# Splitting expert weights two to a call and further ahead, and the order of the scale in differential attention

## Chip, cores and metric

One NeuronCore of a Trainium2 chip runs the whole program in one launch. The metric is device microseconds (us) from the start to the end of one execution; the kernel before has a median of 4869.98 us in three runs. Engines are named as in the profile: PE (TensorE matmul), PEld (its weight loads), DVE (VectorE), ACT (ScalarE), POOL (GpSimd), SP (SyncE, which issues DMAs here).

## What is computed

Two model blocks follow one another. The first has two layers; a layer normalises 1024 tokens (and, in layer 0, a context of 256 tokens too), mixes them (gating, a Fourier mix, differential attention and neighbourhood attention), and runs an expert layer. The second block (a delta rule and latent attention) is not touched. What is touched:

```python
# differential attention, per head: two softmaxes, the second is weighted and subtracted
w = softmax(q0 @ k0.T) - lam * softmax(q1 @ k1.T);  y = w @ v
# expert-choice feed-forward, 16 experts, each takes the 128 grid tokens (and 32 context tokens) that rank highest
h = silu(x_sel @ w_gate[e]) * (x_sel @ w_up[e])
x[sel] += g2 * gate * (h @ w_down[e])
```

All is float32. A product with near-float32 accuracy is made on PE from three float32r products: an operand x is split into xh (x rounded to float32r) and xl (x - xh), and xh·wh + xh·wl + xl·wh is summed.

## The kernel before

The program is written with a tile framework that puts in the semaphores and chooses, at compile time, the order of the instructions on each engine by a priority (the order of the program text) and by readiness in its own model of time. An engine then runs its own list strictly in that order. A pool's `bufs` is the number of buffers behind one tile name; a new tile waits until the oldest one has been read for the last time.

**Experts** (`experts`, from L1110; once per layer, `ctx` is true in layer 0). Each of 16 experts has three 1024x1024 weight matrices, so three products per expert: gate, up and down. The order is: gate 0, up 0, and then for each e: gate e+1, down e, up e+1. `weight` (L1160) brings one half of a matrix: a raw tile `w` of 128 x 4 x 1024 (2 MB) from the SP queue, with three raw buffers (`wraw`, made in `run`), and its split into `wh` and `wl`, two buffers of half a matrix each. The split goes in four quarters of 128x1024: ACT rounds (`wh`, L1165), then DVE subtracts (`wl`, L1166), except for the fourth quarter, whose subtraction goes to POOL. `product` (L1169) calls `weight` at the start of each half, and so the split of a half stands in the program right before the matmuls that need it. In layer 0 the half first runs the context's columns: 16 matmuls that use a 32-column strip of PE each, on the raw float32 `w` (L1181, `ps_c`; the trace has two records for each, 32 per half). Then come the half's 24 main matmuls (L1187, `ps_m`, 512 columns; the trace merges them in pairs).

Around the products stand `fetch` (a gather of the expert's tokens by POOL, and `flip`: four PE transposes into `ps_t`, a rounding on ACT at L1133 and a subtraction on DVE at L1134), `silu` (L1191: ACT tanh and a DVE multiply, after gate), `hidden` (L1199: gate times up and its flip), and `scatter` (L1214: DVE scaling into `rd`, and an accumulating scatter by POOL). `run` (L1223) places their steps between the `yield`s of a product: in layer 0 a product has 16 yields, eight of them in the context's part.

PSUM has eight banks: three `m` tiles of two banks, one `c` and one `t`, in both layers.

**Differential attention** (`diff_unit`, L577). A unit is one head and 128 queries against 1280 keys (256 for the two context units). `a(m)`, for the two maps m = 0, 1, makes scores S on PE (L591), takes a row minimum from PSUM on DVE (`mx`, L592, 128x1280) and the exponential on ACT (L594, into `e0` or `e1`). `b` takes reciprocals (L598), a one-column weight `sm` by a scalar-tensor-tensor (STT, L599), scales `e1` by it (L600), all on DVE, and adds `e0` on POOL (L601). `c` transposes the result on PE (L615) and copies it on ACT; `d` multiplies by v. `units` (L554) is a software pipeline written by hand: in one step the newest unit does a(0), the one before it b, the newest a(1), older ones d and c. There are two S tiles in PSUM. Layer 0 has 40 units (8 of them over 256 keys), layer 1 has 32.

Of the kernel before, what the change touches and what calls it, by code (L numbers as in the profile page):

```python
# [23 lines left out]
NE = 16  # L24
# [38 lines left out]
class Kernel:  # L63
# [490 lines left out]
    def units(self, q, new, steps):  # L554

        for i, u in enumerate(new):
# [3 lines left out]
            if old[0]:  # L560
                old[0]["a"](0)
            if old[1]:
                old[1]["b"]()
            if old[0]:
                old[0]["a"](1)
            for x in (0, 1):
# [10 lines left out]
    def diff_unit(self, p, ps, V, Y, h, Z, t):  # L577
# [6 lines left out]
        def a(m):  # L584
            if m == 0:
                U["mx"] = p.tile([128, 2], F32, name="mx", bufs=4)
                U["sm"] = p.tile([128, 4], F32, name="sm", bufs=6)
            S = ps("S", 3).rearrange("p a b -> p (a b)")
            for c in range(0, nk, 512):
                n = min(512, nk - c)  # L590
                nc.tensor.matmul(S[:, c:c + n], Z[0][m][:, t * 128:(t + 1) * 128], Z[1][m][:, k0 + c:k0 + c + n], start=True, stop=True)  # L591
            nc.vector.tensor_reduce(U["mx"][:, m:m + 1], S[:, :nk], AX.X, OP.min)  # L592
            e = U[m] = p.tile([128, T], F32, name=f"e{m}", bufs=3)
            nc.scalar.activation(e[:, :nk], S[:, :nk], AF.Exp, scale=-1.0, bias=U["mx"][:, m:m + 1], accum_out=U["sm"][:, m:m + 1])  # L594

        def b():
            sm, w = U["sm"], U[1]
            nc.vector.reciprocal(sm[:, 2:4], sm[:, 0:2])  # L598
            nc.vector.scalar_tensor_tensor(sm[:, 3:4], sm[:, 3:4], self.nlam, sm[:, 0:1], op0=OP.mult, op1=OP.mult)  # L599
            nc.vector.tensor_scalar(w[:, :nk], w[:, :nk], sm[:, 3:4], None, op0=OP.mult)  # L600
            nc.gpsimd.tensor_add(w[:, :nk], w[:, :nk], U[0][:, :nk])  # L601
# [37 lines left out]
    def nbr_unit(self, p, ps, V, Y, h, H, i):  # L639
# [34 lines left out]

        def b():
            sm = U["sm"]
# [433 lines left out]
    def experts(self, l):  # L1110
# [4 lines left out]
        quarters = [x.rearrange("t (g c) -> (t g) c", g=4) for x in (self.hc, self.xc)]  # L1115
        with self.pool("ex") as p, self.banks("exps", m=3, c=1, t=1) as ps:
            g2 = p.tile([128, 1024], F32, name="g2")
# [41 lines left out]

            def weight(name, e, half):  # L1160
                w = self.wr.tile([128, 4, 1024], F32, name="w", tag="w")
                nc.sync.dma_start(w, A[name][l, e, half * 512:(half + 1) * 512].rearrange("(k p) f -> p k f", p=128))
                wh, wl = [p.tile([128, 4, 1024], F32R, name=f"w{b}", bufs=2) for b in "hl"]
                for k in range(4):
                    nc.scalar.activation(wh[:, k], w[:, k], AF.Copy)  # L1165
                    (nc.gpsimd if k == 3 else nc.vector).tensor_sub(wl[:, k], w[:, k], wh[:, k].bitcast(F32))  # L1166
                return w, wh, wl

            def product(U, key, x, name, e):  # L1169

                pm = U[key] = ps("m", 2)
                pc = None
                X = U[x]
                for half in range(2):
                    w, *W = weight(name, e, half)
                    if ctx and half == 0:
                        pc = U[key + "c"] = ps("c")
                    for k in range(4 if ctx else 0):
                        b = half * 4 + k
                        for g in range(4):  # L1180
                            nc.tensor.matmul(pc[g * 32:(g + 1) * 32, :256], U[x[0] + "cT"][:, b % 2 * 128 + b // 2 * 32:b % 2 * 128 + b // 2 * 32 + 32],  # L1181
                                             w[:, k, g * 256:(g + 1) * 256], start=b == 0, stop=b == 7)
                        yield
                    for k in range(4):
                        for q, (i, j) in enumerate(((0, 0), (0, 1), (1, 0))):
                            for c in range(2):
                                nc.tensor.matmul(pm[:, c], X[i][:, half * 4 + k], W[j][:, k, c * 512:(c + 1) * 512],  # L1187
                                                 start=half + k + q == 0, stop=half == 1 and k == 3 and q == 2)
                        yield
# [41 lines left out]
            for f in fetch(0):  # L1231
                f()
            run(product(E[0], "g", "xT", "exp_w_gate", 0), [], 0)
            silu(E[0])
            run(product(E[0], "u", "xT", "exp_w_up", 0), fetch(1), 0)
            for e in range(NE):
                U = E[e]
                steps = hidden(U)
                if e + 1 < NE:
                    run(product(E[e + 1], "g", "xT", "exp_w_gate", e + 1), steps, 1)  # L1240
                    silu(E[e + 1])
                else:
                    for f in steps:
                        f()
                run(product(U, "d", "hT", "exp_w_down", e), [], 0)
                scatter(U, e)
                if e + 1 < NE:
                    run(product(E[e + 1], "u", "xT", "exp_w_up", e + 1), fetch(e + 2) if e + 2 < NE else [], 0)

# [1091 lines left out]
```

## Time and profile before

| | |
|---|---|
| median of 3 runs (lowest to highest) | 4869.98 us (4869.22 to 4873.66) |
| the profiled execution's own time | 4872.44 us |
| its span in the trace | 4870.5 us |
| PE / DVE / ACT / POOL busy share of the span | 91% / 65% / 46% / 28% |
| mean granted TensorE clock | 0.952 of full speed |
| layer 0: differential attention, experts | about 392 to 600 us, 948 to 1726 us |
| layer 1: differential attention, experts | about 2050 to 2222 us, 2505 to 3194 us |

Times are counted in us from the start of the span. A group row gives the line, engine, operation, tiles written and read, shapes, count, busy us and mean ns of one, then the idle time of the engine before them and what ended it. A timeline row gives start, duration, engine, line, operation, tiles, count, and in brackets the idle time before it. In both a duration includes any time in which a started instruction was held up.

### The profile page before, as it was taken

Reading aid. Unit: us, or ns where it says so; the run is one execution under the profiler, and the core shown is the slowest. Engines: PE = TensorE matmul, PEld = TensorE weight load, DVE = VectorE, ACT = ScalarE, POOL = GpSimd, SP = SyncE. Lnnn points to the kernel's source line nnn. Section 1 sums busy time; section 2 is a strip of 40 time slices with the busy share of each in tenths; the row PEclk is TensorE's granted clock in tenths of the full one; section 3 lists DMA queues with packets and bytes.
Section 4 is the critical chain, followed back from the end, with each engine's and each line's share of the span. In section 5 each row is a group of like instructions: output and inputs, shape, how many; then the busy total and the mean of one; then the engine's idle time right before and its main releaser. Section 6 shows DMA issues by size and latency. Waiting matters only on the chain.

```text
span 4870.5 us, 77258 instructions
## 1 busy us (share of the span) xinstructions
PE 4427.4 (91%) x30151; PEld 3480.5 (71%) x30151; DVE 3183.5 (65%) x6512; ACT 2225.7 (46%) x4037; POOL 1358.2 (28%) x1033
## 2 busy tenths in 40 slices
PE   8998889799999979989959888879999998898899
PEld 4686676476777757867747666658888876787787
DVE  6536877755555566397778998856666663676551
ACT  3326653255555543376336656643333331454330
POOL 2214502244454422162124444412111100022111
PEclk9999899899999989999979999989999999999999
DMA  6422246687878722313548988821111123146757
GB/s 209 159 89 63 60 140 252 217 295 285 291 285 293 279 87 84 103 48 92 202 160 327 329 320 316 309 95 45 36 36 45 41 61 119 56 169 224 191 151 150
DMA packets 333997, 817.14 MB, mean 168 GB/s; under 512 B 32524, under 2 KB 125380, under 8 KB 333632
## 3 DMA queue, kind: packets, MB, share of 16 engines
q1 hardware_dynamic: 228368, 602.22, 34.2%
q0 software_dynamic: 51520, 125.07, 10.9%
q10 hardware_dynamic: 53744, 84.92, 5.0%
q8 instruction: 237, 3.88, 0.3%
q14 instruction: 128, 1.05, 0.1%
HBM read 690.47 MB, written 121.66 MB: 167 GB/s over the span
## 4 chain that ended last, share of the span: by engine, by line
PE 30%; DVE 8%; issue 5%; ACT 4%; DMA 3%; POOL 1%; SPq 0%; ACTq 0%; POOLq 0%; DVEq 0%
PE ps_z L1358 8%; PE ps_m L1187 5%; DVE wl L1166 4%; ACT wh L1165 2%; PE ps_mm L2211 2%; PE ps_S L2119 2%; PE ps_t L2147 1%; PE ps_m L917 1%; PE ps_i L1680 1%; PE ps_i L1694 1%; PE ps_m L1854 1%; PE ps_i L1687 1%; POOL wl L1166 1%; PE ps_t L1482 1%; PE ps_o L1599 1%
## 5 line engine op out<-in xcount | busy, mean ns | idle before, releaser
L1166 DVE TENSOR_TENSOR wl<-w,wh 128x1024 fp32r<-128x1024 f32 x576 | 843.5, 1508 | 179.7 <-ACT wh L1165 179.7
L1165 ACT ACTIVATE wh<-w 128x1024 fp32r<-128x1024 f32 x768 | 754.6, 1050 | 264.0 <-PE ps_m L1187 151.5
L1166 POOL TENSOR_TENSOR wl<-w,wh 128x1024 fp32r<-128x1024 f32 x192 | 535.7, 2825 | 634.9 <-ACT wh L1165 571.1
L1187 PE MATMUL ps_m<-wl,xTh 128*128 128x512 f32 x1024 | 344.6, 411 | 49.0 <-DVE wl L1166 33.6
L1187 PE MATMUL ps_m<-wh,xTh 128*128 128x512 f32 x1024 | 336.2, 410 | 1.4 <-ACT xTh L1133 1.4
L376 PE MATMUL ps_mm<-wh,hh 128*128 128x256 f32 (+1 forms) x928 | 322.5, 350 | 9.3 <-ACT wh L313 6.1
L1187 PE MATMUL ps_m<-wh,xTl 128*128 128x512 f32 x1024 | 325.1, 399 | 0.0
L376 PE MATMUL ps_mm<-wl,hh 128*128 128x256 f32 (+1 forms) x928 | 317.9, 344 | 2.7 <-DVE wl L314 2.6
L376 PE MATMUL ps_mm<-wh,hl 128*128 128x256 f32 (+1 forms) x928 | 316.1, 342 | 0.0
L1358 PE MATMUL ps_z<-hh,wh 128*128 128x350 f32 (+2 forms) x792 | 277.5, 351 | 2.0 <-ACT hh L1291 1.2
L1187 PEld LDWEIGHTS ps_m<-wl,xTh 128*128 128x128 f32 x1024 | 190.0, 192 | 114.4 <-DVE wl L1166 51.9
L1358 PE MATMUL ps_z<-hl,wh 128*128 128x350 f32 (+3 forms) x792 | 268.1, 339 | 0.0
L1358 PE MATMUL ps_z<-hh,wl 128*128 128x350 f32 (+2 forms) x792 | 264.5, 334 | 0.0
L601 POOL TENSOR_TENSOR e<-e,e 128x1280 f32<-128x1280 f32 (+1 forms) x72 | 191.6, 2661 | 188.2 <-DVE e L600 154.8
L1187 PEld LDWEIGHTS ps_m<-wh,xTh 128*128 128x128 f32 x1024 | 188.0, 192 | 64.2 <-issue 14.4
L1187 PEld LDWEIGHTS ps_m<-wh,xTl 128*128 128x128 f32 x1024 | 195.1, 192 | 41.3
L592 DVE TENSOR_REDUCE mx<-ps_S 128x1 f32<-128x1280 f32 (+1 forms) x144 | 196.1, 1366 | 37.0 <-PE ps_S L591 36.3
L376 PEld LDWEIGHTS ps_mm<-wh,hh 128*128 128x128 f32 x928 | 177.3, 192 | 48.0 <-issue 11.0
L376 PEld LDWEIGHTS ps_mm<-wl,hh 128*128 128x128 f32 x928 | 178.5, 192 | 22.4 <-DVE wl L314 4.4
L594 ACT ACTIVATE e<-ps_S,mx 128x1280 f32<-128x1280 f32 (+1 forms) x144 | 177.4, 1233 | 33.2 <-DVE mx L592 22.0
L376 PEld LDWEIGHTS ps_mm<-wh,hl 128*128 128x128 f32 x928 | 177.5, 192 | 18.8 <-issue 0.8
L1187 PE MATMUL ps_m<-wl,hTh 128*128 128x512 f32 x512 | 165.0, 403 | 20.5 <-DVE wl L1166 12.7
(661 smaller groups left out, 10754.0 us busy)
## 6 DMA issues: line engine op xcount, KB each, us to landing
w<-in_exp_w_gate SPq DMA_DIRECT2D x64, 2048.0 KB
w<-in_exp_w_up SPq DMA_DIRECT2D x64, 2048.0 KB
w<-in_exp_w_down SPq DMA_DIRECT2D x64, 2048.0 KB
w<-in_ada_w SPq DMA_DIRECT2D x12, 2048.0 KB
z<-zd POOLq DMA_DIRECT2D x76, 320.0 KB, 4.6
wraw<-in_ada_w SPq DMA_DIRECT2D x38, 512.0 KB
zd<-hi ACTq DMA_DIRECT2D x76, 256.0 KB
zw<-in_t_win SPq DMA_DIRECT2D x64, 256.0 KB
```

The lines of the kernel that those rows point to most:

```text
L376: nc.tensor.matmul(pm[:, o:], hs[i][x][:, k, a * 128:(a + 1) * 128], w[:, k % 2, o:], start=q == 0, stop=q == 23)
L592: nc.vector.tensor_reduce(U["mx"][:, m:m + 1], S[:, :nk], AX.X, OP.min)
L594: nc.scalar.activation(e[:, :nk], S[:, :nk], AF.Exp, scale=-1.0, bias=U["mx"][:, m:m + 1], accum_out=U["sm"][:, m:m + 1])
L601: nc.gpsimd.tensor_add(w[:, :nk], w[:, :nk], U[0][:, :nk])
L917: nc.tensor.matmul(pm, a[:, k], b[:, k], start=k + x == 0, stop=k == 7 and x == 2)
L1165: nc.scalar.activation(wh[:, k], w[:, k], AF.Copy)
L1166: (nc.gpsimd if k == 3 else nc.vector).tensor_sub(wl[:, k], w[:, k], wh[:, k].bitcast(F32))
L1187: nc.tensor.matmul(pm[:, c], X[i][:, half * 4 + k], W[j][:, k, c * 512:(c + 1) * 512], start=half + k + q == 0, stop=half == 1 and k == 3 ...
L1358: nc.tensor.matmul(q[:M, :n], a[:, k % 4], b[:, k, z0:z0 + n], start=k == 0 and x == 0, stop=k == 7 and x == 2)
L1482: nc.tensor.transpose(pt[:r, i * 128:(i + 1) * 128], src[:, tok(t0 + i)[1]], self.ident)
L2119: nc.tensor.matmul(S[:, ks], q[:, i * 128:(i + 1) * 128], k[:, ks], start=x == 0, stop=x == 4)
L2211: nc.tensor.matmul(pm[:, c], a[:, k], b[:, k, c * 512:(c + 1) * 512], start=k + z == 0, stop=k == 7 and z == 2)
```

## The change

In both layers the fourth quarter's subtraction goes from POOL to DVE, and ACT and DVE handle two quarters (128x2048) with one instruction each: half as many split instructions on ACT, and 192 subtractions per layer on DVE in place of 288 there and 96 on POOL. The splits are traced ahead of their use, over the borders between products: in layer 0 by one half (G = 4, two buffers of a half as before), in layer 1 by three pairs of quarters (G = 2, five buffers of a pair, in all ten quarters in place of eight). Raw loads stay as they are: 2 MB each, three buffers, on SP's queue.

In layer 0 the context's 32 matmuls of a product stand together at its start. They read the raw tiles of both halves, which are therefore held until then. No yield stands among them any more, so the steps of `run` stand between main matmuls only. In layer 1 PSUM's `c` bank, unused there, becomes a second `t`.

In differential attention a step traces a(0), a(1), then b, and the STT and the scale of b are tied behind the newest unit's last row minimum on DVE's list (an ordering at compile time, with no semaphore). Reciprocal and POOL's addition are not tied. Neighbourhood attention's a(1) is empty, so its order stays.

```diff
             if old[0]:
                 old[0]["a"](0)
+                old[0]["a"](1)
             if old[1]:
-                old[1]["b"]()
-            if old[0]:
-                old[0]["a"](1)
+                old[1]["b"](old[0] and old[0].get("max"))
...
-            nc.vector.tensor_reduce(U["mx"][:, m:m + 1], S[:, :nk], AX.X, OP.min)
+            U["max"] = nc.vector.tensor_reduce(U["mx"][:, m:m + 1], S[:, :nk], AX.X, OP.min).ins
...
-        def b():
+        def b(behind):
             sm, w = U["sm"], U[1]
             nc.vector.reciprocal(sm[:, 2:4], sm[:, 0:2])
-            nc.vector.scalar_tensor_tensor(sm[:, 3:4], sm[:, 3:4], self.nlam, sm[:, 0:1], op0=OP.mult, op1=OP.mult)
-            nc.vector.tensor_scalar(w[:, :nk], w[:, :nk], sm[:, 3:4], None, op0=OP.mult)
+
+            with self.tc.issue_after(behind) if behind else nullcontext():
+                nc.vector.scalar_tensor_tensor(sm[:, 3:4], sm[:, 3:4], self.nlam, sm[:, 0:1], op0=OP.mult, op1=OP.mult)
+                nc.vector.tensor_scalar(w[:, :nk], w[:, :nk], sm[:, 3:4], None, op0=OP.mult)
             nc.gpsimd.tensor_add(w[:, :nk], w[:, :nk], U[0][:, :nk])
...
-        with self.pool("ex") as p, self.banks("exps", m=3, c=1, t=1) as ps:
+        with self.pool("ex") as p, self.banks("exps", m=3, **(dict(c=1, t=1) if ctx else dict(t=2))) as ps:
...
-            def weight(name, e, half):
-                w = self.wr.tile([128, 4, 1024], F32, name="w", tag="w")
-                nc.sync.dma_start(w, A[name][l, e, half * 512:(half + 1) * 512].rearrange("(k p) f -> p k f", p=128))
-                wh, wl = [p.tile([128, 4, 1024], F32R, name=f"w{b}", bufs=2) for b in "hl"]
-                for k in range(4):
-                    nc.scalar.activation(wh[:, k], w[:, k], AF.Copy)
-                    (nc.gpsimd if k == 3 else nc.vector).tensor_sub(wl[:, k], w[:, k], wh[:, k].bitcast(F32))
-                return w, wh, wl
+            G, ahead = (4, 1) if ctx else (2, 3)
+            order = [("exp_w_gate", 0), ("exp_w_up", 0)]
+            for e in range(NE):
+                order += [("exp_w_gate", e + 1)] * (e + 1 < NE) + [("exp_w_down", e)] + [("exp_w_up", e + 1)] * (e + 1 < NE)
+            todo = [(name, e, k) for name, e in order for k in range(0, 8, G)]
+            ready = []
+
+            def split():
+                if not todo:
+                    return
+                name, e, k = todo.pop(0)
+                if k % 4 == 0:
+                    self.wraw = self.wr.tile([128, 4, 1024], F32, name="w", tag="w")
+                    nc.sync.dma_start(self.wraw, A[name][l, e, k * 128:(k + 4) * 128].rearrange("(k p) f -> p k f", p=128))
+                w = self.wraw[:, k % 4:k % 4 + G]
+                wh, wl = [p.tile([128, G, 1024], F32R, name=f"w{b}", bufs=ahead + (1 if ctx else 2)) for b in "hl"]
+                for i in range(0, G, 2):
+                    nc.scalar.activation(wh[:, i:i + 2], w[:, i:i + 2], AF.Copy)
+                    nc.vector.tensor_sub(wl[:, i:i + 2], w[:, i:i + 2], wh[:, i:i + 2].bitcast(F32))
+                ready.append((w, wh, wl))
+
+            def weight():
+                split()
+                return ready.pop(0)
+            for _ in range(ahead):
+                split()
...
-                for half in range(2):
-                    w, *W = weight(name, e, half)
-                    if ctx and half == 0:
+                for s in range(0, 8, G):
+                    w, *W = weight()
+                    if ctx and s == 0:
                         pc = U[key + "c"] = ps("c")
-                    for k in range(4 if ctx else 0):
-                        b = half * 4 + k
-                        for g in range(4):
-                            nc.tensor.matmul(pc[g * 32:(g + 1) * 32, :256], U[x[0] + "cT"][:, b % 2 * 128 + b // 2 * 32:b % 2 * 128 + b // 2 * 32 + 32],
-                                             w[:, k, g * 256:(g + 1) * 256], start=b == 0, stop=b == 7)
-                        yield
-                    for k in range(4):
+
+                        for b in range(8):
+                            v = (w, ready[0][0])[b // 4]
+                            for g in range(4):
+                                nc.tensor.matmul(pc[g * 32:(g + 1) * 32, :256], U[x[0] + "cT"][:, b % 2 * 128 + b // 2 * 32:b % 2 * 128 + b // 2 * 32 + 32],
+                                                 v[:, b % 4, g * 256:(g + 1) * 256], start=b == 0, stop=b == 7)
+                    for k in range(G):
+                        b = s + k
                         for q, (i, j) in enumerate(((0, 0), (0, 1), (1, 0))):
                             for c in range(2):
-                                nc.tensor.matmul(pm[:, c], X[i][:, half * 4 + k], W[j][:, k, c * 512:(c + 1) * 512],
-                                                 start=half + k + q == 0, stop=half == 1 and k == 3 and q == 2)
+                                nc.tensor.matmul(pm[:, c], X[i][:, b], W[j][:, k, c * 512:(c + 1) * 512],
+                                                 start=b + q == 0, stop=b == 7 and q == 2)
                         yield
```

## Rows read from the trace of the kernel before

**Rows 1.** Stretches: length, busy us (count) of PE, PEld, DVE, ACT, POOL; clock; DMA share, GB/s
```profile
1000.00:1700.00 700.00, 700.00 (x5191) 492.49 (x5185) 410.29 (x421) 401.79 (x466) 340.78 (x141) 1.00 0.80 287
2540.00:3180.00 640.00, 562.22 (x2392) 427.36 (x2390) 567.47 (x390) 390.49 (x434) 272.31 (x117) 0.97 0.87 317
...
2110.00:2210.00 100.00, 87.78 (x730) 64.60 (x728) 97.58 (x131) 80.43 (x140) 65.52 (x35) 1.00 0.19 46
```

**Rows 2.** DVE's groups by shape, experts of layer 0, then of layer 1
```profile
L1166 DVE TENSOR_TENSOR wl<-w,wh 128x1024 fp32r<-128x1024 f32 x288 | 341.8, 1223 | 159.7 <-ACT wh L1165 159.7
...
L1166 DVE TENSOR_TENSOR wl<-w,wh 128x1024 fp32r<-128x1024 f32 x288 | 501.7, 1792 | 20.0 <-ACT wh L1165 20.0
```

**Rows 3.** Waits in layer 1's experts: us in total, times, longest us
```profile
PEld ps_m L1187 <- DVE wl L1166: 73.8, 73, 4.6
...
ACT wh L1165 <- DMA w<-in_exp_w_up: 1.8, 3, 1.2
```

**Rows 4.** Timeline of SP's queue, layer 1's experts: issues of raw tiles
```profile
2645.53 9.34 SPq L1162 DMA_DIRECT2D w<-in_exp_w_gate  x2
...
2930.90 7.34 SPq L1162 DMA_DIRECT2D w<-in_exp_w_up  x2
...
3111.85 9.26 SPq L1162 DMA_DIRECT2D w<-in_exp_w_gate  x2
```

**Rows 5.** Timeline of ACT, layer 1's experts
```profile
2939.66 3.90 ACT L1165 ACTIVATE wh<-w 128x1024 fp32r<-128x1024 f32 x4 [0.30 <-DMA w<-in_exp_w_up]
```

**Rows 6.** Stretches of 20 us, layer 1's experts (columns as in rows 1)
```profile
2820.00:2840.00 20.00, 16.88 (x65) 12.92 (x64) 17.16 (x11) 6.97 (x8) 8.68 (x4) 0.83 0.99 325
...
2900.00:2920.00 20.00, 16.64 (x63) 12.53 (x64) 18.48 (x12) 8.28 (x9) 9.97 (x5) 0.91 1.01 362
...
2940.00:2960.00 20.00, 15.98 (x68) 11.80 (x67) 18.46 (x11) 11.85 (x13) 11.98 (x6) 1.00 1.00 352
```

**Rows 7.** Timeline of PE, layer 0's experts
```profile
1202.40 0.62 PE L1187 MATMUL ps_m<-wl,hTh 128*128 128x512 f32 x2
...
1206.94 0.61 PE L1187 MATMUL ps_m<-wh,hTl 128*128 128x512 f32 x2
1207.49 1.93 PE L1181 MATMUL ps_c<-w,hcT 128*32 128x256 f32 x32
1209.35 0.73 PE L1187 MATMUL ps_m<-wh,hTh 128*128 128x512 f32 x2
...
1215.02 1.50 PE L1181 MATMUL ps_c<-w,xcT 128*32 128x256 f32 x24
...
1217.61 0.73 PE L1187 MATMUL ps_m<-wh,xTh 128*128 128x512 f32 x2
...
1219.56 0.39 PE L1187 MATMUL ps_m<-wl,xTh 128*128 128x512 f32 x1
...
1220.14 0.48 PE L1187 MATMUL ps_m<-wl,xTh 128*128 128x512 f32 x1
```

**Rows 8.** Timeline of SP's queue, layer 0's experts
```profile
1209.53 8.62 SPq L1162 DMA_DIRECT2D w<-in_exp_w_gate  x2
...
1257.68 8.62 SPq L1162 DMA_DIRECT2D w<-in_exp_w_gate  x2
```

**Rows 9.** DVE's groups by shape, differential attention: layer 0, then twice layer 1
```profile
L599 DVE SCALAR_TENSOR_TENSOR sm<-sm,nlam 128x1 f32<-128x1 f32 x40 | 24.8, 621 | 0.5
...
L592 DVE TENSOR_REDUCE mx<-ps_S 128x1 f32<-128x1280 f32 x64 | 94.8, 1483 | 11.9 <-PE ps_S L591 11.5
...
L599 DVE SCALAR_TENSOR_TENSOR sm<-sm,nlam 128x1 f32<-128x1 f32 x32 | 25.6, 801 | 0.6
```

**Rows 10.** Timelines of POOL and of DVE, layer 1's differential attention
```profile
2117.05 2.91 POOL L601 TENSOR_TENSOR e<-e,e 128x1280 f32<-128x1280 f32 x1 [1.16 <-DVE e L600]
...
2115.68 0.20 DVE L599 SCALAR_TENSOR_TENSOR sm<-sm,nlam 128x1 f32<-128x1 f32 x1
...
2118.38 1.59 DVE L599 SCALAR_TENSOR_TENSOR sm<-sm,nlam 128x1 f32<-128x1 f32 x1
```

More of the change, by code (lines that the diff above doesn't have):

```diff
@@ L1 @@
 import math
-from contextlib import ExitStack, contextmanager
+from contextlib import ExitStack, contextmanager, nullcontext
 from itertools import chain
@@ L673, in a, with b @@
             nc.scalar.activation(e[:, n:n + 256], S[:, 768:], AF.Exp, bias=m, accum_out=sm[:, 2:3])
-        def b():
+        def b(behind):
             sm = U["sm"]
@@ L1169, in product @@
-            def product(U, key, x, name, e):
+            G, ahead = (4, 1) if ctx else (2, 3)
[17 more added lines that the diff above has]
+                ready.append((w, wh, wl))
@@ L1171, in product @@
+            def weight():
[3 more added lines that the diff above has]
+                split()
+            def product(U, key, x):
                 pm = U[key] = ps("m", 2)
-                pc = None
                 X = U[x]
-                for half in range(2):
-                    w, *W = weight(name, e, half)
-                    if ctx and half == 0:
+                for s in range(0, 8, G):
+                    w, *W = weight()
+                    if ctx and s == 0:
@@ L1232, in experts @@
                 f()
-            run(product(E[0], "g", "xT", "exp_w_gate", 0), [], 0)
+            run(product(E[0], "g", "xT"), [], 0)
             silu(E[0])
-            run(product(E[0], "u", "xT", "exp_w_up", 0), fetch(1), 0)
+            run(product(E[0], "u", "xT"), fetch(1), 0)
             for e in range(NE):
@@ L1239, in experts @@
                 if e + 1 < NE:
-                    run(product(E[e + 1], "g", "xT", "exp_w_gate", e + 1), steps, 1)
+                    run(product(E[e + 1], "g", "xT"), steps, 1)
                     silu(E[e + 1])
@@ L1244, in experts @@
                         f()
-                run(product(U, "d", "hT", "exp_w_down", e), [], 0)
+                run(product(U, "d", "hT"), [], 0)
                 scatter(U, e)
                 if e + 1 < NE:
-                    run(product(E[e + 1], "u", "xT", "exp_w_up", e + 1), fetch(e + 2) if e + 2 < NE else [], 0)
+                    run(product(E[e + 1], "u", "xT"), fetch(e + 2) if e + 2 < NE else [], 0)
     def h_src(self, t):
```

## The prediction

> **What bounds it now.** I read the stretches first: they show which engine is full in each of the four stages that the diff touches, and no other stage is touched. In layer 0's experts PE is busy for 700 of 700 us and everything else has room [rows 1]. In layer 1's experts no engine is full on paper: DVE 567 of 640 us, PE 562, transfers 0.87 of their time at 317 GB/s [rows 1]. The reader should then ask what DVE's time consists of. The groups answer it: the same 128x1024 subtraction takes 1.223 us on average in layer 0 and 1.792 us in layer 1 [rows 2]. The difference is not work: in both layers DVE does the same 288. It is time in which DVE's instruction is held while POOL subtracts the fourth quarter. The waits say that PE pays: its weight load waited 73.8 us for DVE's `wl`, while ACT waited only 1.8 us for transfers [rows 3]. So layer 1 is bound by DVE behind POOL, one expert each 42.39 us: gate loads at 2645.53 and, 11 experts on, at 3111.85 [rows 4]. In layer 1's differential attention DVE is busy 97.6 of 100 us [rows 1], and part of that is again holding: the one-column STT takes 0.20 us when free and 1.59 us when POOL's 2.91 us addition has begun before it [rows 10].
>
> **Layer 1's experts.** Removed: POOL's quarter. DVE gets it, so per expert 12 instructions of 128x2048. No row has that shape; its ceiling is two free ones, 2.45 us (from 1.223 [rows 2]), its floor the same less one start, and I take the ceiling as it makes no difference. DVE's other work is 567.47/640 x 42.39 = 37.6 us per expert less 18 x 1.792 = 32.3, so 5.3. Sum for DVE: 12 x 2.45 + 5.3 = 34.7 us. PE: a pair of matmuls costs 0.454 us (ten pairs from 1202.40 to 1206.94 [rows 7]), 72 pairs 32.7, four flips at 0.35 (1219.56 to 1220.14 is 0.58, less half a pair, 0.23 [rows 7]) 1.4, together 34.1. ACT's work was 61% [rows 1] and shrinks. The tracing ahead by three pairs gives PE 3 x 12 x 0.227 = 8.2 us of work in hand at each border between products; the tanh after gate, the scaling into `rd` and the flips are behind those splits on their queues, but nobody needs them before the next product.
>
> Then transfers are late next. They move 317 GB/s x 42.39 us = 13.44 MB per expert. Six stretches of 20 us, from 2600 to 2960, have a share of 0.98 or more; they moved 325 to 362 GB/s, 349 on average [rows 6]. At 349 an expert takes 38.5 us, above DVE and PE. Can three raw buffers keep the transfers going? A raw tile issued at 2930.90, into an empty queue, was there at 2939.66, 8.8 us [rows 4, 5]. It is then held for ACT's first rounding (1.95 us, half of today's four in 3.90 [rows 5]) and two subtractions, 4.9. Together 15.65 us, against 3 x 38.5/6 = 19.2 us that three buffers allow: yes. I take 38.9, with 1% for gaps. Gain: (42.39 - 38.9) x 16 = 56 us. Bounds: no gain if loads come no denser than today; (42.39 - 13.44/0.362) x 16 = 84 us at the best stretch. The second `ps_t` bank only loosens flips and counts as nothing.
>
> The Trainium skill ("SBUF — State Buffer", A bandwidth-pool intuition that's wrong) says that a core gets about 358 GB/s of HBM and that this is nearly always the limit. By it an expert would take an estimated 37.5 us and the layer gain 78; rows 6 reach its figure in one stretch only.
>
> **Layer 0's experts.** PE is full, so only PE's time counts; POOL's quarter and the wider splits cost nothing while PE covers them: DVE is at 410 and ACT at 402 of 700 us [rows 1], and DVE's share rises to some 12 x 2.45 + 6 = 35 us of 46. What PE saves: a half takes 7.53 us (1207.49 to 1215.02 [rows 7]), of which 12 pairs are 5.45, so the context costs 2.08. Its records cost (1.93 - 1.50)/8 = 0.054 us each [rows 7], 32 of them 1.72, so each entry into the narrow strips and back costs 0.36. Two bunches become one: 0.36 per product, 1.08 per expert. And two flips per expert now stand inside a bunch: from 1215.02 to 1217.61 it takes 2.59 us, against 1.86 (1207.49 to 1209.35) without; the 0.73 becomes 0.35 among main matmuls [rows 7]. Twice 0.38 is 0.76. Together 1.84 per expert, 29 us for 16. Bounds: 0 to 40.
>
> The cover: both raw halves are now held until the bunch, so only one buffer is loading then. The next product's second half is issued when the bunch ends, 3.8 us into a product of 15.4 (48.15 us per expert before [rows 8], less 1.84, over 3); it lands 8.8 us later, at 12.6, and is first read half way through the next bunch, at 17.2. That leaves 4.6 us. Its SP queue holds nothing else; gathers and scatters are on POOL's, which gets free.
>
> **Differential attention.** The STT's holding is (621 - 205) x 40 = 16.6 us in layer 0 and (801 - 205) x 32 = 19.1 us in layer 1, with 0.205 for a free one [rows 9, 10]. After the change two row minima stand before it; they read PSUM and last 1.483 us each [rows 9], 2.97 together against POOL's 2.91, so POOL is done. In layer 1 the period is 5.0 us per unit, DVE's without holding 4.28, and PE comes next with 87.78/20 = 4.39 [rows 1]. I take 4.5: 0.5 x 32 = 16 us. In layer 0 the two small units per head break the pattern and DVE has idle time; I take half, 8 us. Sum 24. Added: scale and POOL's addition come one row minimum later, and transposes wait for the addition. If PE pays half a microsecond for that per unit, 36 us are lost; bounds -10 to 36, as the transposes belong to a unit one step older.
>
> The Trainium skill ("SBUF — State Buffer", SBUF: two separate sides) says that the port pair of VectorE and GpSimd is a lock held for a whole instruction, by VectorE operations with two SBUF inputs or in a two-port mode. By that rule only POOL's end counts: if its later start keeps pace with the later STT, STT and scale are held as before, and the sum below is 85 in place of 109.
>
> **Sum.** 56 + 29 + 24 = 109 off the profiled 4872.4 gives 4763; that execution is 2.5 above the median, so **4761 us** against 4870.
>
> **Rivals.**
> *Transfers keep up better.* Experts of layer 1 at 37.1 us: 84 + 29 + 24 = 137, **4733**. For it: the stretch with 362 GB/s. Against: 325 at the same share. Chance 0.18.
> *Loads come no denser.* If the share of 0.87 is what gathers, scatters and buffers allow, layer 1 stays at 42.39 us, and 53 are left: **4817**. Against: SP waited for buffers, as ACT hardly ever waited for data. Chance 0.15.
> *The bunch waits for its second raw half.* If that load queues behind another, it takes 8.8 + 6.0 (2.1 MB at 349 GB/s), landing at 18.6, 1.4 late in each of 48 products: 67 lost, **4828**. Chance 0.12.
> *The reorder buys nothing* (additions come as much later as row minima come earlier): 85, **4785**. Chance 0.08.
> *DVE was not held by POOL but is slow when transfers are dense.* This one ends slower. Then 1.792 stays per 1024 columns: 24 x 1.792 + 5.3 = 48.3 us per expert, 5.9 x 16 = 95 lost against 53 won elsewhere: **4912**. It decides from 1.68 us per 1024 columns up, where an expert takes 45.7. Against it: layer 0 has 287 GB/s [rows 1] and 1.223 us. Chance 0.07.
>
> **Chances.** The forecast keeps 0.40. The range leaves out the slow rival and the waiting bunch, 0.19 together, and reaches from the best transfers with all of the holding gone (4733 less 12, less some us for layer 0's upper bound) to the case without denser loads: 4712 to 4825. About 0.2%, 10 us, is what a measurement can tell from no change: faster 0.91, same 0.03, slower 0.06.
>
> **What would show it.** In layer 1's experts: no POOL subtraction, a mean of at most 2.5 us for 128x2048 on DVE, a DMA share of 0.95 or more, ACT's waits ending on `w` loads, an expert each 38 to 39.5 us. In layer 0: 64 records of `ps_c` in a row, flips only between `ps_m` pairs, PE full, 46.3 us per expert. In differential attention: STT at 0.2 us everywhere, 4.5 us per unit in layer 1. It is wrong if `wl` stays near 1.8 us per 1024 columns, if PE waits for `w` at a product's start in layer 0, or if PE waits for POOL's additions.

## The result, and the profile after

The kernel after takes **4739.59 us** (median of four runs, 4736.78 to 4749.64), the kernel before 4870.88 on the same chip: a ratio of 0.9734, 95% interval 0.9717 to 0.9750. The profiled execution took 4737.11 us, 135.3 less than the profiled one of before. It lies inside the forecast range, 21 us below the forecast of 4761. Of the experiments below, e2 and e3 each had one execution far out (10523.59 and 14343.81 us); their medians in the table include it, their ratios leave it out.

The page's first part now reads:

```profile
PE 4364.9 (92%) x30151; PEld 3489.2 (74%) x30151; DVE 3178.7 (67%) x6320; ACT 2192.2 (46%) x3653; POOL 913.3 (19%) x841
```

PE has the same work in less time; POOL fell from 28% to 19%. Where the time came from, by the two kernels' traces (experts: from the first to the last `wh,xTh` matmul of gate and up; attention: from the first to the last score matmul):

| stretch | before | after | gain | predicted |
|---|---|---|---|---|
| differential attention, layer 0 | 193.7 | 195.4 | -1.7 | 8 |
| experts, layer 0 | 754.5 | 732.3 | 22.2 | 29 |
| differential attention, layer 1 | 159.1 | 152.1 | 7.0 | 16 |
| experts, layer 1 | 663.2 | 561.6 | 101.6 | 56 |
| borders and all other stages | | | 6.2 | 0 |

So the sum came out larger than 109 because one term was nearly twice as large, while three others were smaller. Most of the last row belongs to the attention's reorder too, as e10 below shows.

**Layer 1's experts.** The views of stretches (columns as in rows 1), of the DVE group, of waits from 2560 to 2990 us (us in total, times, longest), and of SP's queue:

```profile
2600.00:2700.00 100.00, 95.48 (x437) 76.94 (x435) 87.77 (x56) 68.61 (x49) 8.26 (x5) 1.00 1.00 371
2700.00:2800.00 100.00, 97.97 (x450) 80.35 (x448) 90.39 (x56) 69.23 (x46) 21.30 (x5) 1.00 1.01 379
2800.00:2900.00 100.00, 97.23 (x445) 79.24 (x444) 91.93 (x57) 71.10 (x48) 21.84 (x6) 1.00 1.01 378
```

```profile
L1182 DVE TENSOR_TENSOR wl<-w,wh 128x2048 fp32r<-128x2048 f32 x143 | 320.0, 2284 | 40.8 <-ACT wh L1181 40.8
```

```profile
ACT wh L1181 <- DMA w<-in_exp_w_gate: 45.5, 19, 4.7
...
ACT wh L1181 <- DMA w<-in_exp_w_up: 40.2, 20, 5.1
PEld ps_m L1209 <- DVE wl L1182: 21.5, 22, 1.6
ACT wh L1181 <- DMA w<-in_exp_w_down: 12.9, 13, 1.9
PE ps_m L1209 <- DVE wl L1182: 12.5, 19, 1.2
```

```profile
1054.34 0.37 SPq L1177 DMA_DIRECT2D w<-in_exp_w_gate  x1
...
1614.85 0.37 SPq L1177 DMA_DIRECT2D w<-in_exp_w_gate  x1
...
2555.67 0.37 SPq L1177 DMA_DIRECT2D w<-in_exp_w_gate  x1
...
2989.94 0.37 SPq L1177 DMA_DIRECT2D w<-in_exp_w_gate  x1
```

Twelve experts lie between the issues of each pair. Layer 1: (2989.94 - 2555.67) / 12 = **36.19 us** per expert, against 42.39 [rows 4]. A subtraction of twice the size takes 2.284 us, where a single one took 1.792 [rows 2]. This points to the loads in place of DVE as the bottleneck (e5 and e8 test it): ACT, which hardly ever waited for them [rows 3], now waits 98.6 us of 430, and they move 371 to 379 GB/s where they moved 317 [rows 1].

**Layer 0's experts.** PE is full (700.00 of 700 us from 960 to 1660), and an expert takes (1614.85 - 1054.34) / 12 = **46.71 us**, against 48.15 [rows 8]. PE's timeline shows a flip among main matmuls and a product between its own bunch and the next one's:

```profile
1255.72 0.62 PE L1209 MATMUL ps_m<-wh,xTl 128*128 128x512 f32 x2
1256.18 0.60 PE L1132 MATMUL ps_t<-ident,x 128*128 128x128 f32 x4
1256.54 0.71 PE L1209 MATMUL ps_m<-wh,xTh 128*128 128x512 f32 x2
1257.09 0.63 PE L1209 MATMUL ps_m<-wl,xTh 128*128 128x512 f32 x2
...
1280.36 3.66 PE L1203 MATMUL ps_c<-w,hcT 128*32 128x256 f32 x64
1283.95 0.73 PE L1209 MATMUL ps_m<-wh,hTh 128*128 128x512 f32 x2
...
1295.08 3.66 PE L1203 MATMUL ps_c<-w,xcT 128*32 128x256 f32 x64
```

The 64 records stand in a row and take 3.59 us. From bunch to bunch this flip-free product takes 14.72 us; two halves of before took 15.06 (twice 7.53, [rows 7]).

**Differential attention.** The STT's group in layer 0 and in layer 1, then the score matmuls of both layers (count, duration ns min/median/max, first to last start), then the stretches that answer to the last line of rows 1, for layer 0 and for layer 1:

```profile
L600 DVE SCALAR_TENSOR_TENSOR sm<-sm,nlam 128x1 f32<-128x1 f32 x40 | 22.1, 554 | 0.3
...
L600 DVE SCALAR_TENSOR_TENSOR sm<-sm,nlam 128x1 f32<-128x1 f32 x32 | 8.6, 267 | 0.3
```

```profile
L590 PE MATMUL ps_S<-z x208: 276/415/797, 390.6 to 586.0; 96*128 96x512 f32 x64, 96*128 96x256 f32 x40
...
L590 PE MATMUL ps_S<-z x192: 276/398/797, 2021.8 to 2173.9; 96*128 96x512 f32 x128, 96*128 96x256 f32 x64
```

```profile
395.00:580.00 185.00, 160.25 (x1103) 119.56 (x1102) 151.02 (x231) 131.94 (x240) 102.63 (x57) 0.83 0.18 41
2075.00:2175.00 100.00, 92.30 (x774) 68.86 (x770) 89.52 (x137) 85.36 (x148) 68.31 (x36) 1.00 0.20 46
```

In layer 1 every STT but the last takes 0.21 or 0.22 us, DVE goes from 97.6 to 89.5 of 100 us, and a unit takes 152.1/32 = 4.75 us where it took 5.0. In layer 0 most of the holding stayed (621 to 554 ns [rows 9]), and the scores' stretch is no shorter; its granted clock in this execution is 0.83, and 0.87 in the same stretch of before.

### The profile page after: what moved, and what is told of

The parts are those of the page before. It is cut to its first block, busy times and chain, and to the rows that moved or that the text cites. A ratio compares the mean times of both kernels' runs of the same rounds, so it can differ in the third digit from the quotient of the medians.

```text
span 4735.3 us, 76064 instructions
## 1 busy us (share of the span) xinstructions
PE 4364.9 (92%) x30151; PEld 3489.2 (74%) x30151; DVE 3178.7 (67%) x6320; ACT 2192.2 (46%) x3653; POOL 913.3 (19%) x841
## 4 chain that ended last, share of the span: by engine, by line
PE 27%; DVE 9%; DMA 7%; issue 6%; ACT 2%; POOL 0%; SPq 0%; ACTq 0%; POOLq 0%; DVEq 0%
PE ps_z L1380 8%; DVE wl L1182 4%; PE ps_mm L2233 2%; DMA w<-in_exp_w_gate 2%; PE ps_S L2141 2%; DMA w<-in_exp_w_down 2%; PE ps_m L1209 1%; PE ps_t L2169 1%; PE ps_m L918 1%; PE ps_m L1876 1%; PE ps_i L1702 1%; PE ps_i L1716 1%; PE ps_i L1709 1%; ACT wh L1181 1%; DMA w<-in_b_w_out 1%
## 5 line engine op out<-in xcount | busy, mean ns | idle before, releaser
L1182 DVE TENSOR_TENSOR wl<-w,wh 128x2048 fp32r<-128x2048 f32 x384 | 862.2, 2286 | 205.6 <-ACT wh L1181 203.5
L1181 ACT ACTIVATE wh<-w 128x2048 fp32r<-128x2048 f32 x384 | 717.7, 1910 | 311.4 <-PE ps_m L1209 179.6
L1209 PE MATMUL ps_m<-wl,xTh 128*128 128x512 f32 x1024 | 324.9, 396 | 7.4 <-DVE wl L1182 7.4
L1242 POOL DMA_INDIRECT xd<-rd,idx x32 | 115.2, 3598 | 412.6 <-DVE rd L1241 382.6
```

Of the source, the lines that this page charges most:

```text
L1181: nc.scalar.activation(wh[:, i:i + 2], w[:, i:i + 2], AF.Copy)
L1182: nc.vector.tensor_sub(wl[:, i:i + 2], w[:, i:i + 2], wh[:, i:i + 2].bitcast(F32))
L1209: nc.tensor.matmul(pm[:, c], X[i][:, b], W[j][:, k, c * 512:(c + 1) * 512], start=b + q == 0, stop=b == 7 and q == 2)
L1242: nc.gpsimd.indirect_dma_start(out=dst, out_offset=bass.IndirectOffsetOnAxis(ap=idx[:, e:e + 1], axis=0), in_=r, in_offset=None, compute_o ...
```

## The experiments

These are eleven runs on two chips. All ratios are against the kernel before on the same chip (4862.07, 4866.10 and 4864.01 us in the three groups), with 95% intervals. The last two columns are the period of one expert in steady state, in us. The kernel after had 36.19 and 46.71 in its first profile and 36.55 and 46.72 in e10, so a difference of 0.4 us in layer 1 is no more than two executions of one kernel show.

| run | us | ratio | layer 1 | layer 0 |
|---|---|---|---|---|
| e1 reorder alone | 4844.27 | 0.9966 (0.9954 to 0.9978) | 42.35 | 48.17 |
| e2 POOL's quarter back | 4800.47 | 0.9868 (0.9850 to 0.9886) | 40.08 | 46.9 |
| e3 quarter to DVE alone | 4778.68 | 0.9818 (0.9800 to 0.9836) | 37.02 | 48.13 |
| e4 context by halves | 4752.49 | 0.9771 (0.9756 to 0.9787) | 36.18 | 47.61 |
| e5 half the loads | 4707.29 | 0.9674 (0.9659 to 0.9689) | 34.53 | 46.71 |
| e6 no tie | 4755.02 | 0.9773 (0.9759 to 0.9786) | 36.52 | 46.73 |
| e7 one pair ahead | 4749.90 | 0.9759 (0.9744 to 0.9774) | 37.71 | 46.72 |
| e8 four raw buffers | 4715.27 | 0.9690 (0.9675 to 0.9705) | 34.54 | 46.72 |
| e9 two raw buffers | 4899.98 | 1.0079 (1.0063 to 1.0094) | 46.37 | 46.73 |
| e10 the kernel after again | 4735.98 | 0.9730 (0.9717 to 0.9744) | 36.55 | 46.72 |
| e11 e8 again | 4714.68 | 0.9688 (0.9675 to 0.9701) | 34.54 | 46.72 |

### What freed layer 1: e2 and e3

e2 puts the fourth quarter back on POOL in the new kernel:

```diff
-                    nc.vector.tensor_sub(wl[:, i:i + 2], w[:, i:i + 2], wh[:, i:i + 2].bitcast(F32))
+                    if (k + i) % 4 == 2:
+                        nc.vector.tensor_sub(wl[:, i], w[:, i], wh[:, i].bitcast(F32))
+                        nc.gpsimd.tensor_sub(wl[:, i + 1], w[:, i + 1], wh[:, i + 1].bitcast(F32))
+                    else:
+                        nc.vector.tensor_sub(wl[:, i:i + 2], w[:, i:i + 2], wh[:, i:i + 2].bitcast(F32))
```

> The new kernel with the fourth quarter's subtraction back on POOL in both layers, splits still traced ahead. Theory A (DVE held by POOL is what bound layer 1, and nothing else frees it): layer 1 goes from 36.2 back to about 42 us per expert, 4737 + 5.9 x 16 = about 4830, DVE's subtractions held again to some 1.8 us per 1024 columns. Theory B (the waits at the borders between products were the loss; DVE was only 89% busy, and work traced ahead fills that): 38 to 39 us per expert, about 4775. Both: layer 0 stays at 46.7 us per expert, as PE covers it.

e3 takes the quarter from POOL in the kernel before, and does nothing else:

```diff
-                    (nc.gpsimd if k == 3 else nc.vector).tensor_sub(wl[:, k], w[:, k], wh[:, k].bitcast(F32))
+                    nc.vector.tensor_sub(wl[:, k], w[:, k], wh[:, k].bitcast(F32))
```

> The kernel before with the fourth quarter's subtraction on DVE, nothing else changed: single quarters, no tracing ahead. Theory A (the holding is the loss): DVE's mean returns to 1.22 us per quarter, DVE's work falls to 34.7 us per expert, layer 1 goes from 42.4 to about 37.5, 80 us won: about 4790. Theory B (the borders are the loss): the mean falls as well, but PE still waits for wl at each product's start, and layer 1 stays at 40.5 to 42, 4840 to 4865. Both: layer 0 stays at 48.1, as PE is full.

From 2560 to 2960 us, e2's two DVE groups and its stretch (columns as in rows 1), then e3's:

```profile
L1186 DVE TENSOR_TENSOR wl<-w,wh 128x2048 fp32r<-128x2048 f32 x60 | 198.4, 3307 | 13.2 <-ACT wh L1181 13.2
L1183 DVE TENSOR_TENSOR wl<-w,wh 128x1024 fp32r<-128x1024 f32 x60 | 134.5, 2242 | 0.0
...
2560.00:2960.00 400.00, 363.32 (x1610) 287.31 (x1610) 384.59 (x202) 252.89 (x173) 230.46 (x81) 0.99 0.94 342
```

```profile
L1166 DVE TENSOR_TENSOR wl<-w,wh 128x1024 fp32r<-128x1024 f32 x259 | 301.0, 1219 | 22.3 <-ACT wh L1165 22.1
...
2560.00:2960.00 400.00, 388.24 (x1743) 307.60 (x1742) 362.03 (x348) 283.68 (x314) 35.05 (x22) 1.00 1.00 369
```

With POOL's quarter back, DVE is held again (3.307 us for what takes 2.284, 2.242 for what takes 1.219) and is busy 96% of the time; tracing ahead, with the wider instructions, then wins 2.3 us of the 6.2 per expert, and e2 ends between its two theories. Without POOL's quarter and without tracing ahead, 5.4 us of the 6.2 are won, 86 us over 16 experts. Theory A holds in the main: the holding was the loss. The two parts overlap, so their single gains (43 and 89 us of the stretch in the table above) don't add up to 102. e3 also settles the rival in which DVE is slow by itself when transfers are dense: at 369 GB/s a quarter takes 1.219 us.

### What bounds layer 1 now: e5, e7, e8, e9

e5 loads one half of each matrix in layer 1 and splits it twice, so it leaves out the second half of every matrix there:

```diff
-                if k % 4 == 0:
+                if k % (4 if ctx else 8) == 0:
```

> The new kernel with half of layer 1's weight loads: each product splits the first half of its matrix twice, so layer 1 leaves out the second half of every weight matrix; the splits and matmuls stay as many. Theory (transfers bind layer 1 now): the expert falls from 36.2 to PE's 34.1 or DVE's some 33 plus small gaps, 34.2 to 34.8 us, 22 to 32 us in all, and ACT no longer waits for loads. Rival (DVE and PE bind, transfers are only dense): 36.2 stays, less than 5 us.

```profile
2600.00:2900.00 300.00, 300.00 (x1390) 248.58 (x1389) 286.51 (x175) 223.58 (x149) 54.14 (x17) 1.00 0.63 214
```

In this stretch PE is full, an expert takes 34.53 us, and ACT waits for no load. So transfers were what kept the new kernel at 36.2. PE's sum of 34.1 in the prediction was 0.4 too low, which is what four flips at 0.46 in place of 0.35 would make (0.46 is layer 0's, measured below).

e7 lowers the depth of the split (`G, ahead = (2, 1)` in layer 1 in place of `(2, 3)`, three buffers of a pair in place of five):

> The new kernel with layer 1's splits traced one pair ahead in place of three (three buffers of a pair in place of five). Theory (the holding was the loss, loads bind now, and tracing ahead only has to cover DVE's other work at the borders): 36.2 to 37.0 us per expert, up to 13 us lost, no more than the kernel before with the quarter on DVE showed (37.0). Rival (the depth is what makes the loads dense): 38 or more, 30 us lost.

It took 37.71 us, more than the theory allowed and less than the rival wanted; against the kernel after (0.9734) it is some 0.25% slower, though the two intervals overlap (0.9744 to 0.9774 and 0.9717 to 0.9750), so the loss rests on the period. PE's waits for `wl` grow from 34.0 (21.5 + 12.5 in 430 us) to 56.6 us in 400:

```profile
PEld ps_m L1209 <- DVE wl L1182: 35.2, 34, 2.0
...
PE ps_m L1209 <- DVE wl L1182: 21.4, 31, 1.6
```

I had left out that it holds fewer split buffers than the kernel before (six quarters, not eight). Which of the two costs the time, the depth or the buffers, this run can't tell.

e8 gives up one pair of split buffers for a fourth raw buffer:

```diff
-            G, ahead = (4, 1) if ctx else (2, 3)
+            G, ahead = (4, 1) if ctx else (2, 2)
...
+            count = iter(range(1000))
...
-                    self.wraw = self.wr.tile([128, 4, 1024], F32, name="w", tag="w")
+                    fourth = not ctx and next(count) % 4 == 3
+                    self.wraw = p.tile([128, 4, 1024], F32, name="w4", bufs=1) if fourth else self.wr.tile([128, 4, 1024], F32, name="w", tag="w")
```

> The new kernel with a fourth raw buffer in layer 1, in the room of one pair's split (two pairs ahead in place of three). Theory A (the transfers are at their ceiling of some 372 GB/s with three raw buffers): 36.2 us per expert, no change. Theory B (the rate depends on how many loads are on their way, and a share near 1 is no ceiling): more than 372 GB/s and 34.5 to 35.5 us per expert, 10 to 27 us won.

```profile
2660.00:2760.00 100.00, 100.00 (x466) 82.81 (x465) 93.98 (x58) 72.33 (x50) 13.06 (x6) 1.00 1.03 393
2760.00:2860.00 100.00, 100.00 (x463) 82.72 (x462) 93.97 (x58) 73.20 (x48) 12.11 (x5) 1.00 1.03 395
```

```profile
2620.71 7.11 SPq L1179 DMA_DIRECT2D w<-in_exp_w_gate  x2
...
2966.10 7.13 SPq L1179 DMA_DIRECT2D w<-in_exp_w_gate  x2
```

Theory B holds: 393 to 395 GB/s, PE full, (2966.10 - 2620.71) / 10 = 34.54 us between gate issues, the same as with half of the loads left out. The 371 to 379 GB/s of the kernel after was no ceiling.

e9 goes the other way, two raw buffers with one pair ahead:

```diff
-            G, ahead = (4, 1) if ctx else (2, 3)
+            G, ahead = (4, 1) if ctx else (2, 1)
...
-                    self.wraw = self.wr.tile([128, 4, 1024], F32, name="w", tag="w")
+                    self.wraw = self.wr.tile([128, 4, 1024], F32, name="w", tag="w") if ctx else p.tile([128, 4, 1024], F32, name="w2", bufs=2)
```

> The new kernel with two raw buffers in layer 1 and splits one pair ahead; to be read beside the run with three raw buffers and one pair ahead (37.5 us per expert, 363 GB/s). Theory (the rate of the loads follows from how many are on their way): a tile takes 8.8 us to land in an empty queue and is then held for a rounding and two subtractions, 1.9 + 2 x 2.29, so two buffers make 2 loads in 15.3 us, 45.9 us per expert and some 290 GB/s, about 135 us more than with three, 4885. Rival (the memory's rate is the limit, and it is reached with two loads as with three): 37 to 39 us per expert, 4750 to 4775.

```profile
2541.10 7.13 SPq L1177 DMA_DIRECT2D w<-in_exp_w_gate  x2
...
3097.51 5.08 SPq L1177 DMA_DIRECT2D w<-in_exp_w_gate  x2
```

```profile
2760.00:2860.00 100.00, 86.11 (x352) 66.65 (x351) 69.60 (x42) 52.78 (x35) 7.96 (x4) 0.93 0.82 296
```

(3097.51 - 2541.10) / 12 = 46.37 us, where 45.9 was expected (and 4899.98 us in all, where 4885 was). Two, three and four raw buffers give some 296, 362 (e7) and, with one pair more ahead, 394 GB/s. As long as nothing else is slower (with four, PE is full), the pace of the loads is the number of buffers over the time that one is loaded and held.

### Layer 0: e4

e4 gives each half its own bunch again, without a yield in it:

```diff
-                    if ctx and s == 0:
-                        pc = U[key + "c"] = ps("c")
-
-                        for b in range(8):
-                            v = (w, ready[0][0])[b // 4]
+                    if ctx and s == 0:
+                        pc = U[key + "c"] = ps("c")
+                    if ctx:
+                        for b in range(s, s + 4):
                             for g in range(4):
...
-                                                 v[:, b % 4, g * 256:(g + 1) * 256], start=b == 0, stop=b == 7)
+                                                 w[:, b % 4, g * 256:(g + 1) * 256], start=b == 0, stop=b == 7)
```

> The new kernel with layer 0's context columns in two bunches of 32 records, one per half, still without a yield among them, so that flips stay between main matmuls. Theory (each entry into the narrow strips and back costs 0.36 us): 48 entries more, 1.08 us per expert, 46.7 to 47.8, 17 us in all: 4754. Rival (the bunch buys nothing, the flips' new place is all of the gain): 46.7 and 4737. Second rival (raw tiles freed earlier let the loads keep up better): less than 4737.

PE's timeline, a flip-free product from its first bunch to the next product's:

```profile
1279.66 1.93 PE L1202 MATMUL ps_c<-w,hcT 128*32 128x256 f32 x32
1281.53 0.73 PE L1208 MATMUL ps_m<-wh,hTh 128*128 128x512 f32 x2
...
1287.19 1.93 PE L1202 MATMUL ps_c<-w,hcT 128*32 128x256 f32 x32
...
1294.72 1.93 PE L1202 MATMUL ps_c<-w,xcT 128*32 128x256 f32 x32
```

15.06 us against 14.72: an entry more costs 0.34 us (0.36 was said). An expert takes 47.61 us, 0.90 more than in the new kernel (1.08 expected), and 14 us over 16 experts. The other 0.54 us of the 1.44 won is left for the flips' new place.

### Differential attention: e1, e6, e10

e1 is the kernel before with the attention's part of the diff alone:

> The kernel before with the new order of differential attention alone. Theory (the holding goes, but the ring of two S tiles and PE take most of what DVE gains): layer 1 goes from 5.0 to 4.75 us per unit, the STT's mean there from 0.80 to about 0.27 us, layer 0 gains 2 or 3 us; together about 10 us, 4860. The size as predicted: 4.5 us per unit and 24 us, 4846. Rival (the reorder buys nothing, what the new kernel shows there comes from elsewhere): 4870, 5.0 us per unit.

It won 0.34%, 16.5 us (11 to 22), where the theory said about 10 and the prediction 24. Layer 1's scores go from 159.1 to 150.9 us, 4.72 us per unit. Layer 0's stretch became shorter by 6.4 us, at a granted clock of 0.92:

```profile
L590 PE MATMUL ps_S<-z x208: 276/400/794, 390.4 to 577.7; 96*128 96x512 f32 x64, 96*128 96x256 f32 x40
...
395.00:580.00 185.00, 155.64 (x1160) 115.00 (x1160) 157.95 (x245) 136.66 (x254) 106.90 (x59) 0.92 0.18 43
```

e6 keeps the new order in the program and drops the tie:

```diff
-            with self.tc.issue_after(behind) if behind else nullcontext():
+            with nullcontext():
```

> The new kernel with a(0), a(1), b in the new order in the program but without the tie of STT and scale behind the newest row minimum. Theory (the tie keeps the STT clear of POOL's addition): the STT is held again, some 0.7 us on average in layer 1, the unit goes back from 4.75 to about 5.0 us, 8 to 16 us lost. Rival (the order in the program is enough): 4.75 and no change. Second rival (the tie costs, as scale and addition come late): a few us won.

```profile
L600 DVE SCALAR_TENSOR_TENSOR sm<-sm,nlam 128x1 f32<-128x1 f32 x32 | 17.8, 556 | 0.7
...
L590 PE MATMUL ps_S<-z x192: 276/397/797, 2026.9 to 2186.0; 96*128 96x512 f32 x128, 96*128 96x256 f32 x64
```

Layer 1's scores take 159.1 us again, exactly as before the change, and the ratio rises from 0.9734 to 0.9773. The loss, some 19 us, is more than the 8 to 16 expected and more than layer 1's 7.0; e10 takes that up. So the tie makes the gain, and the order in the program alone makes none here. The holding came back only in part (a mean of 556 ns, against 801 before), yet all of layer 1's gain is gone: the length doesn't go in proportion to the holding.

e10 is the kernel after itself, to see its attention in layer 0 a second time:

> The new kernel itself once more, on the chip of the run beside it. Layer 1's experts at 36.2 us each and layer 0's at 46.7 again, as their clock is granted in full. Differential attention in layer 0 as its granted clock falls out: 195.4 us at 0.83, 185 to 187 at 0.92 to 0.94, so between 4728 and 4745 in all. Rival (the length of that stage has nothing to do with the clock): 195 us whatever the clock.

```profile
L590 PE MATMUL ps_S<-z x208: 276/398/797, 393.0 to 584.0; 96*128 96x512 f32 x64, 96*128 96x256 f32 x40
...
395.00:580.00 185.00, 155.25 (x1108) 114.60 (x1109) 153.54 (x236) 134.75 (x245) 102.52 (x57) 0.89 0.19 46
```

191.0 us at a clock of 0.89, where the same program took 195.4 at 0.83. Over all runs with the tie the stretch goes with the clock: 195.5 us at 0.83 (e5, e7), 190.3 and 189.8 at 0.89 (e8, e9), 188.6 and 190.0 at 0.90 (e2, e11), 187.3 at 0.92 (e1), 185.4 at 0.94 (e4). Without it the stretch took 193.7 at 0.87, 191.0 at 0.86 (e3) and 194.6 at 0.85 (e6), which is about where the runs with the tie lie at such a clock. So in this stretch no gain can be told from the spread that goes with the clock. That the clock sets the length is read from the runs side by side; no run set it, and whether the tie also moves the clock stays open.

But the stretch ends with the last score. Behind it, neighbourhood attention's first score comes sooner with the tie. Here are both score matmuls in layer 0, before and then after (the first line of after stands above, 390.6 to 586.0):

```profile
L591 PE MATMUL ps_S<-z x208: 276/415/797, 392.5 to 586.2; 96*128 96x512 f32 x64, 96*128 96x256 f32 x40
L662 PE MATMUL ps_S<-z x208: 277/282/615, 593.3 to 702.1; 128*128 128x256 f32 x88, 128*128 128x320 f32 x16
...
L663 PE MATMUL ps_S<-z x208: 276/282/616, 590.0 to 696.2; 128*128 128x256 f32 x88, 128*128 128x320 f32 x16
```

This gap is 7.1 us before and 4.0 after. It is 6.7 to 7.1 us in the three executions without the tie (before, e3, e6) and 4.0 to 4.6 in the ten with it; in layer 1 it is 5.4 to 5.7 and 3.9 to 4.0. From layer 0's first score to its experts' first matmul the three without the tie take 563.3 to 564.0 us, and the ten with it 550.7 to 562.4, 556.0 on average. So layer 0 does gain, between 1 and 13 us. The mean gain, 7.6 us, and the 7 to 8 us of layer 1's scores come near what e1 won (16.5) and e6 lost (19). How much of layer 0's gain is the tie and how much the clock isn't separated.

### A version that beats both: e11

e8 once more, beside e10 on one chip:

> The version with four raw buffers and two pairs ahead in layer 1 once more, to be set against the new kernel on one chip. Theory: 34.5 us per expert as PE is full, 20 to 25 us below the new kernel, some 0.45%. Rival (the two were told apart by their chips): less than 0.2%.

4714.68 us against 4735.98: 21.3 us or 0.45% faster than the kernel after, with intervals that don't touch (0.9675 to 0.9701 against 0.9717 to 0.9744). A fourth raw buffer, paid for with one pair of split buffers, removes ACT's waits for loads in layer 1's steady state.

## Why the prediction was right, and where its terms were off

**DVE held by POOL (right).** The chain of reasoning from 1.223 against 1.792 us [rows 2] to "the difference is not work" is what e2 and e3 show from both sides. DVE's work per expert, 12 x 2.284 + 5.3 = 32.7 us, is 90% of 36.19, as the stretches show; the ceiling of 2.45 us was on the safe side.

**Layer 1's transfers (mechanism right, size wrong).** The step that failed is "At 349 an expert takes 38.5 us". I took stretches with a share of 0.98 or more [rows 6] for the rate that the memory gives at its best. They moved what the kernel before had asked for. A share near 1 isn't a ceiling: 369 GB/s went with 1.00 (e3), 379 with 1.01, 395 with 1.03 (e8). The term was 56 us and measured 102, more than the bound of 84. The Trainium skill ("SBUF — State Buffer", A bandwidth-pool intuition that's wrong) gives about 358 GB/s for a core, as half of what one memory stack gives two cores. This program runs on one core, and the runs held 371 to 379 and, with four buffers, 393 to 395 over 100 us each, so that figure was no limit here. By my own sum the rival "transfers keep up better" (37.1 us per expert, 4733) came nearest to the result: its mechanism happened, and went further than its price. That the total still came within 21 us of the forecast is in part luck: this term was 46 us too small, and the terms for layer 0's experts and the attention were some 25 too large in the table.

**Three raw buffers, "yes" (half right).** The cycle of one buffer was well built from 8.8 us of landing and the hold: e9 ran at 2 x 46.37/6 = 15.46 us per buffer, where 15.3 was expected from it and 15.65 stood in the prediction. But loads that overlap land later than one in an empty queue: in the kernel after, a half issued at 2742.82 was rounded from 2753.45 on, as soon as it had landed, 10.6 us later (the half before it took 8.8). With three buffers a cycle takes 3 x 36.19/6 = 18.1 us, so a buffer is also held longer (7.5 to 9.3 us) than the 6.9 reckoned, and ACT waits. I compared 15.65 with the 19.2 that an assumed rate allowed, when the cycle and the number of buffers set the rate.

**Tracing ahead (a term left out).** The prediction gave it no price of its own. Together with the wider instructions and the other buffers it was worth 0.8 us per expert beside e3 (37.02 against 36.19), or 0.5 against e10's 36.55; no run tried these parts one by one.

**Layer 0 (right, flips mis-sized).** The bunch's term was 1.08 us per expert: its flip-free product is 0.34 shorter, 1.02 for three, and e4 lost 0.90. The flips' term was 0.76, and 0.42 to 0.54 is left for it of the 1.44 won: "the 0.73 becomes 0.35 among main matmuls" failed. A flip there takes 0.46 us (1256.18 to 1257.09 is 0.91, less a pair of 0.454), as the first pair after it is late too. So 46.71 us in place of 46.3. PE stayed full, so the bunch never waited for its second raw half, and that rival fell.

**Differential attention (mechanism right in layer 1, size wrong).** "POOL is done" holds there: the row minima of 1.48 us put STT and scale behind POOL's addition, and without the tie part of the holding is back (e6). The unit takes 4.75 us, not 4.5. DVE is at 89.5% and PE at 92.3% now, so neither is full; PE's waits before scores are for ACT's exponential, which gives back one of two S tiles (kernel after, 2075 to 2175 us):

```profile
PEld ps_S L590 <- ACT e L593: 10.1, 20, 0.9
...
PE ps_S L590 <- ACT e L593: 5.6, 11, 0.7
```

That this ring of two tiles sets the 4.75 is argued from these rows, and no run tried it. In layer 0 the step "I take half" failed as a mechanism: holding of 14.0 us of 16.6 is left ((554 - 205) x 40 ns). It sits in eight STTs of 1.33 to 2.67 us, two in each head, beside the 256-key units; their row minima of 0.4 us are too short to outlast a 2.9 us addition. What layer 0 gained all the same came by other ways (the shorter gap behind the last score and, perhaps, the clock), so its nearness to the predicted 8 us is luck. An STT of the new kernel there, and the addition of POOL that holds it, in their timelines:

```profile
434.89 2.48 DVE L600 SCALAR_TENSOR_TENSOR sm<-sm,nlam 128x1 f32<-128x1 f32 x1
...
434.45 2.90 POOL L602 TENSOR_TENSOR e<-e,e 128x1280 f32<-128x1280 f32 x1 [1.31 <-PE ps_t L616]
```

Both end at 437.4. By the lock of the Trainium skill ("SBUF — State Buffer", SBUF: two separate sides), held for a whole instruction, only POOL's end counts, and the trace agrees.

**What the rival with loads no denser missed.** It put the share of 0.87 down to gathers, scatters and buffers. They are the same in e3, and the share is 1.00.

## What to carry to other kernels

When one engine's instruction has two mean durations in two stages at the same size, look for what holds it before counting its work; giving the work back to the engine that is held can be cheaper than sharing it. For streamed weights, don't take a rate at a DMA share near 1 for the memory's ceiling: add up landing (with loads overlapping) and holding for one buffer, divide by the number of buffers to get the time per load, and try one buffer more. A reorder in the program text bought no time by itself here, where a scheduler places instructions; the tie to a long instruction did it, and it freed the held instruction only where the long one lasts as long as the work that must be outlasted. And when a stretch is measured from first to last of one instruction, look at what comes behind it too: part of the attention's gain lay there.

## What the runs showed of the hardware

- One core moved 393 to 395 GB/s over 100 us with four buffers for loads of 2 MB, at a DMA share of 1.03.
- Subtracting 2048 columns at once takes 2.284 us, 0.15 less than twice 1.219.
- POOL's scatter instruction was slower where DVE's instructions were longer: in layer 1's experts 2.07 us on average (12 of them) in e3, where DVE subtracts 1024 columns at a time, and 4.09 us (12) in the kernel after, where it subtracts 2048 (3.36 to 3.57 in e5, e7 and e8). That the one causes the other is not shown. DVE is busy about nine tenths of the time in both. It cost nothing, as nobody waits for it there.
- The same program's attention in layer 0 was granted 0.83 of the clock in one execution and 0.89 in another, and took 195.4 and 191.0 us; in layer 1 the clock was 1.00 in both kernels. What differs was not found.
